# Small TensorE work at fixed steps, key products on GpSimd, and the last value pages outside TensorE, in a hybrid decoder step

## The chip, the cores and the metric

The kernel runs on one core of a Trainium2 chip. The metric is the device time of one execution, in microseconds. The time before the change is the median of three runs, 1570.15 us (1565.2 to 1571.04). PE is TensorE, DVE is VectorE, ACT is ScalarE, Pool (POOL in the rows, G in the code) is GpSimd, and SP is the queue that issues all transfers.

## What is computed

One layer of a decoder step over two inputs at once: a prompt of 512 tokens and eight sample sequences of one new token each. All data is 32-bit.

```
z = rmsnorm(x) @ w_in                      # 2048 -> 7168: q, k, v, gate_a, conv halves, gate_c
o = (softmax(q1 k1) - lam * softmax(q2 k2)) @ v      # 8 heads, two maps of 64 each
o_att  = rmsnorm(o) * silu(gate_a)
o_conv = (silu(layernorm(depthwise_conv31(glu))) @ w_pw) * silu(gate_c)
h = x + concat(o_att, o_conv) @ w_out
h = h + sigmoid(rmsnorm(h) @ w_pg) * (p @ w_ple)
y = rmsnorm(h)
```

For the prompt the keys and values are its own. For each of the eight samples they are 4096 cached positions, found through a page table as 32 pages of 128 positions, with 8 heads of 128 columns: a key page and a value page of 512 KB each. That makes 256 key pages and 256 value pages, some 268 MB of the 424 MB that the kernel moves.

## The kernel before

The program is straight-line code, and its order is worked out while it is built. A `Planner` keeps a predicted clock for each engine (`clk["PE"]`, `"V"` for DVE, `"A"` for ACT, `"G"` for Pool, `"Q"` for SP) and a predicted ready time of each tile. Every instruction goes through `Engine`, which records it at line 209 (so every row of the profile says L209; the tiles tell the rows apart).

The spine is a loop over slots (`run_slot`). A slot holds two 128-row blocks of a weight matrix, 512 columns wide, in one `raw` tile of 512 KB. ACT rounds each block to `hi`, Pool subtracts to get `lo = raw - hi`, and PE multiplies activations (split alike into `aht` and `alt`) with both: three matmuls for each of four token tiles, for each of the two blocks. This is the dense work, into the tiles `acc`. Three `hi`/`lo` pairs exist (`HIB`). After each three dense matmuls the loop calls `hook(n)`, with n from 0 to 7 within a slot. The hook issues loads (`wpump` for the slots' weights; `kring.pump`, `vring.pump` for pages), advances the queued generators in `tasks` (attention of the prompt, convolution, norms, softmax, sample work) as far as the planned clocks allow, and ends with `decode_tick(n)`. A generator that is about to use PE yields `on("PE", tiles)`, which holds it until the tiles are ready 500 ns before PE's planned clock.

`decode_tick` handles the pages. For a key page, DVE multiplies it in place with the query row `qb`, spread over 128 partitions, and the products are summed over 64 columns, either by one DVE reduce or, where DVE is planned more than 400 ns late, by sixteen ACT instructions with an accumulator (`k_act`). After 32 pages comes `softmax(s)`, which gives the weights `aw`. The keys of sequence s wait for the softmax of s - 2, and that softmax for the values of s - 4. For a value page, `v_pages` issues eight PE instructions (four column groups of 32 partitions) that add `aw x page` to the persistent PSUM tile `pers`; it takes them when two pages are there, or one at n = 7. `v_end(s)` gathers the result into `oS`.

Two rings hold pages: `kring` with five tiles (`kt`), `vring` with two (`vt`). The key ring takes keys as long as any are left, then values; the value ring takes values from the start. Both then take the `tail` pages: the weights of `w_out` and `w_pg` that the eight samples need after all their values are done (`sample_tail`, `tail_pass`). The slots' weights serve the samples too (`samp`, at n = 7 of every second slot, into `pers`). The last slots of `w_pg` wait until the samples have passed `w_out` (`us2_done`).

In the planner, Pool holds the SBUF port that it shares with DVE for each of its instructions, and so does a DVE instruction with two SBUF inputs. An instruction of one of them that meets one of the other is planned behind it.

Of the kernel before, what the change touches and what calls it, by code (L numbers as in the profile page):

```python
# [16 lines left out]
NSEQ = 8  # L17
# [43 lines left out]
class Planner:  # L61
# [4 lines left out]
    NEAR = dict(PE=0, V=125, A=125, G=60, Q=0)  # L66

    def __init__(self):
        self.t = dict(PE=0.0, V=0.0, A=0.0, G=0.0, Q=0.0, D=0.0)
        self.hist = {}  # L70
        self.late = dict(V=[], G=[])

# [88 lines left out]
    def put(self, eng, fn, args, kw, cost=None):  # L161
# [53 lines left out]
def hymba_step(ctx, tc, x_prompt, x_sample, p_prompt, p_sample, cache_k, cache_v, state_conv, page_table,  # L215
# [122 lines left out]

    def hook(n=7):
        wpump()  # L340
# [161 lines left out]
    def v_end(s):  # L502
# [7 lines left out]
        if vper[0] == s:  # L510
# [18 lines left out]
            yield from gather(ps)  # L529
        ended[0] += 1  # L530
# [6 lines left out]
    K_LATE = 400  # L537
# [8 lines left out]
    def decode_tick(at):  # L546
        if not dec["on"]:
            return
        now = clk["PE"]
        while True:  # L550
            more = k_next()
            pend = dec["pend"]
            if pend and (len(pend) > 1 or not more):
                s, pg, kt = pend[0]
                if k_act_live[0] < 1 and clk["A"] <= now + 300 and clk["V"] > now + K_LATE and plan.ready(kt) <= now + 800:
                    pend.pop(0)
                    k_act_live[0] += 1
                    spawn(k_act(s, pg, kt), rank=2)
                elif clk["V"] <= now + 400:
                    pend.pop(0)  # L560
                    V.tensor_reduce(out=dec["sc"][s][:, pg, :], in_=kt.rearrange("p (x d) -> p x d", d=64), axis=AX.X, op=ADD)
                    k_did(s, kt)
                else:
                    break
            elif more and clk["V"] <= now + 400:
                s, pg = divmod(dec["ik"], NPAGE)
                if pg == 0:
                    dec["sc"][s] = scp.tile([128, NPAGE, 16], F32, tag="sc", name="sc")
                kt, _ = kring.get()
                V.tensor_tensor(out=kt, in0=kt, in1=qbt[s], op=MUL)  # L570
                pend.append((s, pg, kt))
                dec["ik"] += 1
                if pg == NPAGE - 1 and s + 1 < NSEQ:
                    spawn(prep_qb(s + 1), rank=0)
            else:
                break
        v_pages(at == 7)
# [12 lines left out]

    def v_pages(tiled):

        n = v_here()
        if n < (1 if tiled else 2):
            return
# [11 lines left out]
        if vdone[s] == NPAGE:  # L607
            spawn(v_end(s), rank=0)
# [1114 lines left out]
```

## Time and profile before

| | |
|---|---|
| median of 3 runs | 1570.15 us (1565.2 to 1571.04) |
| the profiled execution, its own time | 1576.48 us |
| its span, first to last instruction | 1574.6 us |
| mean granted clock of TensorE | 0.978 |
| PE busy | 1482.9 us, 94% |
| DVE busy | 1100.8 us, 70% |
| ACT busy | 811.7 us, 52% |
| Pool busy | 622.9 us, 40% |
| moved | 424.40 MB, mean 270 GB/s |

Busy shares of the whole span hide the stages, so the rows below cut it where the work changes: the keys run until 1335 us, the last values until 1487 us, and behind that comes the samples' tail. The matmuls of PE overlap in the records: back-to-back dense matmuls start 0.234 us apart while each lasts 0.4 us. PE's work is therefore read from starts, not from durations.

### The profile page before, as it was taken

What the parts mean: (1) busy time and instruction counts of PE and PEld (TensorE: products, weight loads), DVE (VectorE), ACT (ScalarE), POOL (GpSimd) and SP (SyncE); (2) the same over time, 40 slices, a digit from 0 to 9 for tenths busy, and PEclk for the clock granted to TensorE, in tenths of its full rate; (3) what the DMA queues carried; (4) which work ended last, traced back from release to release, by engine and by line L of the source; (5) the groups of instructions that cost most, each with busy time, mean ns of one, the idle gap of its engine ahead of it and who ended that gap; (6) DMA issues with size and microseconds to landing.
All of it is one profiled execution on the core that took longest, in us unless ns stands there. A gap on an engine that the chain in (4) does not pass through costs nothing.

```text
span 1574.6 us, 32145 instructions
## 1 busy us (share of the span) xinstructions
PE 1482.9 (94%) x10448; PEld 1039.5 (66%) x10448; DVE 1100.8 (70%) x1636; ACT 811.7 (52%) x3810; POOL 622.9 (40%) x471
## 2 busy tenths in 40 slices
PE   5899999999999999999999999999999999999786
PEld 4676767666667766677777667766767777665453
DVE  5168987788798978888888868878867888301201
ACT  4156666556655645562445567665655765414202
POOL 5144534323333433344443454434423365425312
PEclk8999999999999999999999999999999999999877
DMA  7648779767887876543358687599878799899997
GB/s 287 233 169 294 273 257 358 275 228 256 320 282 279 296 251 207 188 135 124 126 168 295 228 307 254 187 350 340 299 258 332 275 327 382 306 328 337 395 320 255
DMA packets 148921, 424.40 MB, mean 270 GB/s; under 512 B 14192, under 2 KB 16226, under 8 KB 148480
## 3 DMA queue, kind: packets, MB, share of 16 engines
q1 hardware_dynamic: 148752, 422.35, 75.7%
q8 instruction: 82, 1.34, 0.3%
q14 instruction: 87, 0.71, 0.1%
HBM read 413.62 MB, written 9.63 MB: 269 GB/s over the span
## 4 chain that ended last, share of the span: by engine, by line
PE 75%; DMA 11%; DVE 5%; POOL 3%; issue 3%; ACT 2%; SPq 1%; POOLq 0%; ACTq 0%; DVEq 0%
PE acc L209 57%; PE pers L209 11%; PE misc L209 7%; DMA raw<-in_w_in_dram 4%; POOL lo L209 2%; DVE kt L209 1%; DMA raw<-in_w_out_dram 1%; DMA kt<-in_w_out_dram 1%; DMA raw<-in_w_pg_dram 1%; DVE bt L209 1%; DMA vt<-in_cache_v_dram 1%; DVE sc L209 1%; DMA kt<-in_w_pg_dram 1%; DMA kt<-in_cache_v_dram 0%; ACT hi L209 0%
## 5 line engine op out<-in xcount | busy, mean ns | idle before, releaser
L209 POOL TENSOR_TENSOR lo<-raw,hi 128x512 fp32r<-128x512 f32 x392 | 557.7, 1435 | 829.7 <-ACT hi L209 775.1
L209 ACT CAST hi<-raw 128x512 fp32r<-128x512 f32 x392 | 236.6, 618 | 437.1 <-PE acc L209 218.1
L209 DVE TENSOR_TENSOR kt<-kt,qb 128x1024 f32<-128x1024 f32 x256 | 363.9, 1436 | 41.1 <-DMA kt<-in_cache_k_dram 36.7
L209 PE MATMUL acc<-hi,aht 128*128 128x512 f32 x896 | 377.8, 422 | 7.8 <-ACT hi L209 7.5
L209 PE MATMUL acc<-lo,aht 128*128 128x512 f32 x896 | 360.9, 403 | 17.5 <-POOL lo L209 17.5
L209 PE MATMUL acc<-hi,alt 128*128 128x512 f32 x896 | 357.9, 399 | 0.2 <-DVE alt L209 0.2
L209 ACT ACTIVATE kt<-kt 128x64 f32<-128x64 f32 x1392 | 336.1, 244 | 25.2 <-DVE kt L209 25.2
L209 ACT ACTIVATION_READ_ACCUMULATOR kt<-kt 128x1 f32 x1392 | 262.2, 188 | 0.0
L209 PE MATMUL acc<-aht,hi 128*128 128x512 f32 x576 | 245.6, 426 | 3.9 <-DVE bt L209 3.4
L209 PE MATMUL acc<-aht,lo 128*128 128x512 f32 x576 | 228.8, 397 | 4.5 <-POOL lo L209 4.4
L209 PEld LDWEIGHTS acc<-hi,aht 128*128 128x128 f32 x896 | 170.2, 190 | 92.8 <-issue 32.4
L209 PE MATMUL acc<-alt,hi 128*128 128x512 f32 x576 | 227.5, 395 | 0.0
L209 PEld LDWEIGHTS acc<-lo,aht 128*128 128x128 f32 x896 | 170.7, 190 | 68.4 <-POOL lo L209 28.3
L209 DVE TENSOR_REDUCE sc<-kt 128x16 f32<-128x1024 f32 x169 | 203.4, 1210 | 1.3
L209 PEld LDWEIGHTS acc<-hi,alt 128*128 128x128 f32 x896 | 171.2, 191 | 33.3 <-DVE alt L209 0.7
L209 DVE SCALAR_TENSOR_TENSOR misc<-ft,wdwT,misc 128x512 f32<-128x512 f32 x240 | 180.3, 751 | 6.2
L209 PEld LDWEIGHTS acc<-aht,hi 128*128 128x128 f32 x576 | 108.5, 188 | 65.0 <-issue 34.3
L209 PEld LDWEIGHTS acc<-aht,lo 128*128 128x128 f32 x576 | 108.2, 188 | 34.8 <-POOL lo L209 9.2
L209 PEld LDWEIGHTS acc<-alt,hi 128*128 128x128 f32 x576 | 108.6, 189 | 18.0 <-issue 0.2
L209 PE MATMUL pers<-vt,aw 128*8 128x256 f32 x1624 | 113.4, 380 | 6.3 <-DVE pers L209 5.0
L209 DVE SCALAR_TENSOR_TENSOR acc<-acc,ct 128x512 f32<-128x512 f32 x16 | 11.2, 699 | 128.9 <-ACT acc L209 128.9
L209 PEld LDWEIGHTS pers<-vt,aw 128*8 128x8 f32 x1624 | 31.8, 88 | 62.9 <-issue 32.5
(259 smaller groups left out, 1283.2 us busy)
## 6 DMA issues: line engine op xcount, KB each, us to landing
kt<-in_cache_k_dram SPq DMA_DIRECT2D x256, 512.0 KB
vt<-in_cache_v_dram SPq DMA_DIRECT2D x203, 512.0 KB
raw<-in_w_in_dram SPq DMA_DIRECT2D x112, 512.0 KB
kt<-in_cache_v_dram SPq DMA_DIRECT2D x53, 512.0 KB
raw<-in_w_pg_dram SPq DMA_DIRECT2D x40, 512.0 KB
raw<-in_w_out_dram SPq DMA_DIRECT2D x32, 512.0 KB
kt<-in_w_in_dram SPq DMA_DIRECT2D x12, 512.0 KB
kt<-in_w_out_dram SPq DMA_DIRECT2D x12, 512.0 KB
```

The lines of the kernel that those rows point to most:

```text
L209: real(*args, **kw)
```

## The change

Three things are changed, and the planner's prices with them.

1. A PE step of a generator (`on("PE", ...)`) and `v_pages` go ahead only if `turn()` holds: at n = 3 and n = 7 of a slot, instead of at any n. In a `settle` (the loop waits for something) n counts as 7. The planner adds 92 ns whenever PE goes from dense to other work or back, and prices a group of four column-group matmuls at 226 ns instead of 284 ns, a value page at 431 ns instead of 430 to 580 ns.
2. `decode_tick` may give a key page's product to Pool: if DVE is planned more than 700 ns behind PE's clock, Pool's planned clock is at least 100 ns in the past, and fewer than three multiplied pages wait for their sums. Of the waiting pages it takes the first whose product is due within 700 ns, instead of the oldest.
3. When the last key page of the last sequence has been multiplied, the tile `qb` becomes an accumulator `vacc` for one sequence at a time. `v_aside` then takes arrived value pages: Pool multiplies one with its weights by one instruction with a broadcast operand, or ACT by eight (`v_act`), and DVE adds it to `vacc`. While this is possible, `v_pages` uses PE only if four pages are there. `v_end` sums `vacc` over partitions with sixteen more PE instructions.

The core of the diff:

```diff
+    TURN = 92
...
+            if eng == "PE":
+                dense = outs[0].name.startswith("acc")
+                c += self.TURN if dense != self.dense else 0
+                self.dense = dense
...
-        return lambda: (eng == "PE" or clk[eng] <= clk["PE"] + back) and all(plan.ready(x) <= clk["PE"] + back for x in aps)
+        return lambda: (eng != "PE" or turn()) and (eng == "PE" or clk[eng] <= clk["PE"] + back) and all(plan.ready(x) <= clk["PE"] + back for x in aps)
...
+    def turn():
+        return not main_on[0] or step[0] % TURNS == TURNS - 1
+    TURNS = 4
     def hook(n=7):
+        step[0] = n
...
+        if s in vacc:
+            ps = yield from take("misc")
+            V.memset(ps[:, 0:256], 0.0)
+            yield on("PE", ps[:, 0:256], vacc[s])
+            for h in range(8):
+                a, g = h // 4, h % 4
+                mm(ps[32 * g:32 * g + 8, a * 128:(a + 1) * 128], cst[:, C_ROW + 7 - s:C_ROW + 15 - s],
+                   vacc[s][:, h * 128:(h + 1) * 128], start=False, stop=True, cost=7 if g else 205)
+            va_free.append(plan.ready(vacc.pop(s), True))
+            yield from gather(ps)
...
-    K_LATE = 400
+    K_LATE, K_POOL = 400, -100
...
+            x = next((x for x in pend if plan.ready(x[2]) <= now + 700), None)
+            if x and (len(pend) > 1 or not more):
+                s, pg, kt = x
+                if k_act_live[0] < 1 and clk["A"] <= now + 300 and clk["V"] > now + K_LATE:
...
+            eng = V if clk["V"] <= now + 400 else G if clk["G"] <= now + K_POOL and clk["V"] > now + 700 and len(pend) < 3 else None
+            if eng is None:
+                break
...
-                V.tensor_tensor(out=kt, in0=kt, in1=qbt[s], op=MUL)
+            eng.tensor_tensor(out=kt, in0=kt, in1=qbt[s], op=MUL)
...
+            elif pg == NPAGE - 1:
+                va_free.append(plan.ready(qbt[s], True))
+        v_aside()
+        v_pages(at == 7)
...
+    def v_aside():
+        now = clk["PE"]
+        while v_pend and clk["V"] <= now + 500 and v_pend[0][0] in va_has and plan.ready(v_pend[0][1]) <= now + 600:
+            s, vt, ring = v_pend.pop(0)
+            V.tensor_tensor(out=vacc[s], in0=vacc[s], in1=vt, op=ADD)
+            ring.done(vt)
+            v_did(s)
+        while True:
+            ring = v_ring(600)
+            s, pg = divmod(dec["iv"], NPAGE)
+            if ring is None or not dec["soft"][s] or plan.ready(aw[s % 2]) > now + 500 or not (s in vacc or va_free) or len(v_pend) > 2:
+                return
+            eng = G if clk["G"] <= now + 200 else A if clk["A"] <= now + 300 and v_act_live[0] < 1 else None
+            if eng is None:
+                return
...
+            if eng is G:
+                a = aw[s % 2]
+                G.tensor_tensor(out=out.rearrange("p (h d) -> p h d", d=128), in0=vt.rearrange("p (h d) -> p h d", d=128),
+                                in1=a[:, pg, :].rearrange("p (h o) -> p h o", o=1).to_broadcast([128, 8, 128]), op=MUL, cost=1855)
+                v_made(s, vt, ring, first)
+            else:
+                v_act_live[0] += 1
+                spawn(v_act(s, pg, vt, ring, out, first), rank=2)
+    def v_act(s, pg, vt, ring, out, first):
+        for h in range(8):
+            c = slice(h * 128, (h + 1) * 128)
+            yield lambda: clk["A"] <= clk["PE"] + 400
+            A.activation(out=out[:, c], in_=vt[:, c], func=AF.Copy, scale=aw[s % 2][:, pg, h:h + 1])
...
+    V_MANY = 4
...
-        if n < (1 if tiled else 2):
+        if n < (V_MANY if s_aside() else 1 if tiled else 2) or not turn():
             return
...
-                   start=False, stop=True, cost=20 if cg else 370 + (0 if k or tiled else 150))
+                   start=False, stop=True, cost=7 if cg else 410)
```

## Rows read from the trace of the kernel before

**Rows 1.** The page, part 1: busy time, share of the span and instructions of an engine.

```profile
PE 1482.9 (94%) x10448; PEld 1039.5 (66%) x10448; DVE 1100.8 (70%) x1636; ACT 811.7 (52%) x3810; POOL 622.9 (40%) x471
```

**Rows 2.** The view by windows, cut by stage: the window, its length, busy us (instructions) of PE, PEld, DVE, ACT and POOL, the granted clock, the DMA share and GB/s.

```profile
82.00:560.00 478.00, 462.89 (x3089) 328.69 (x3088) 398.92 (x627) 280.00 (x1441) 186.26 (x137) 1.00 0.78 272
560.00:800.00 240.00, 233.20 (x1592) 166.86 (x1593) 199.24 (x384) 117.28 (x496) 92.48 (x77) 1.00 0.50 170
800.00:1000.00 200.00, 194.60 (x1271) 138.66 (x1269) 163.18 (x197) 117.59 (x565) 87.71 (x59) 1.00 0.71 245
1000.00:1335.00 335.00, 327.06 (x2067) 235.69 (x2066) 270.05 (x281) 207.99 (x1113) 144.50 (x98) 0.99 0.87 314
1335.00:1487.00 152.00, 144.04 (x1055) 87.54 (x1053) 27.32 (x54) 49.55 (x121) 66.84 (x54) 1.00 0.93 340
1487.00:1518.00 31.00, 19.59 (x298) 12.36 (x300) 5.80 (x19) 1.42 (x6) 1.35 (x2) 0.56 0.96 358
1518.00:1575.00 57.00, 40.95 (x570) 26.32 (x562) 8.22 (x18) 12.87 (x25) 14.40 (x13) 0.83 0.79 265
```

**Rows 3.** The view of waits for SP's queue, 82 to 1335 us: who waited for whom, us in total, times, longest us.

```profile
SPq L209 <- PE pers L209: 358.0, 117, 14.0
SPq L209 <- DVE sc L209: 73.2, 45, 12.4
```

**Rows 4.** The same view for PE, 82 to 1335 us.

```profile
PE acc L209 <- POOL lo L209: 12.3, 22, 1.4
```

**Rows 5.** Groups of instructions over the whole span, shapes kept apart: count, busy us, mean ns of one, then the idle time before them.

```profile
L209 POOL TENSOR_TENSOR lo<-raw,hi 128x512 fp32r<-128x512 f32 x392 | 557.7, 1435 | 829.7 <-ACT hi L209 775.1 <-PE acc L209 29.2 <-PE pers L209 20.9
L209 DVE TENSOR_TENSOR kt<-kt,qb 128x1024 f32<-128x1024 f32 x256 | 363.9, 1436 | 41.1 <-DMA kt<-in_cache_k_dram 36.7 <-ACT qb L209 3.5
L209 ACT ACTIVATE kt<-kt 128x64 f32<-128x64 f32 x1392 | 336.1, 244 | 25.2 <-DVE kt L209 25.2
L209 ACT ACTIVATION_READ_ACCUMULATOR kt<-kt 128x1 f32 x1392 | 262.2, 188 | 0.0
L209 DVE TENSOR_REDUCE sc<-kt 128x16 f32<-128x1024 f32 x169 | 203.4, 1210 | 1.3
L209 ACT ACTIVATE o<-misc,arz 128x128 f32<-128x128 f32 x32 | 11.8, 368 | 1.1
L209 POOL TENSOR_TENSOR ft<-ft,stat 128x512 f32<-128x512 f32 x6 | 6.3, 1066 | 0.0
```

**Rows 6.** The timeline of PE at three places: start us, us, instructions merged where equal.

```profile
701.86 0.27 PE L209 MATMUL misc<-cst,o 128*128 128x128 f32 x1
701.89 0.47 PE L209 MATMUL acc<-aht,hi 128*128 128x512 f32 x1
...
1340.50 0.40 PE L209 MATMUL acc<-hi,alt 128*128 128x512 f32 x1
1340.74 0.39 PE L209 MATMUL acc<-lo,aht 128*128 128x512 f32 x1
1341.06 1.05 PE L209 MATMUL pers<-vt,aw 128*8 128x256 f32 x16
1342.04 0.50 PE L209 MATMUL acc<-hi,aht 128*128 128x512 f32 x1
1342.38 0.40 PE L209 MATMUL acc<-hi,alt 128*128 128x512 f32 x1
...
1480.49 0.62 PE L209 MATMUL pers<-kt,aw 128*8 128x256 f32 x8
1480.92 0.61 PE L209 MATMUL pers<-vt,aw 128*8 128x256 f32 x8
```

**Rows 7.** The timeline of PE, 444 to 470 us: the first and the last of the five stretches of value pages in it.

```profile
446.71 1.07 PE L209 MATMUL pers<-vt,aw 128*8 128x256 f32 x16
...
467.95 1.05 PE L209 MATMUL pers<-vt,aw 128*8 128x256 f32 x16
```

**Rows 8.** The view by windows for the instructions that touch the softmax weights `aw` (on PE, eight for each value page): the window, its length, busy us (instructions) of PE, PEld and DVE, then granted clock, DMA share and GB/s of everything.

```profile
505.00:657.00 152.00, 17.35 (x256) 5.17 (x256) 0.43 (x1) 1.00 0.68 237
657.00:814.00 157.00, 0.00 (x0) 0.00 (x0) 0.41 (x1) 1.00 0.42 140
814.00:962.00 148.00, 17.54 (x256) 5.38 (x256) 0.00 (x0) 1.00 0.80 279
962.00:1017.00 55.00, 0.00 (x0) 0.00 (x0) 0.14 (x1) 1.00 0.49 161
...
1335.00:1487.00 152.00, 39.83 (x600) 12.37 (x600) 0.42 (x1) 1.00 0.93 340
```

**Rows 9.** The view by tile for `qb`, 1325 to 1340 us: instruction, count, ns min/median/max, first and last start us, shapes.

```profile
L209 DVE TENSOR_TENSOR kt<-kt,qb x5: 1216/1217/1373, 1325.4 to 1333.8; 128x1024 f32<-128x1024 f32 x5
```

**Rows 10.** The timeline of all engines near 990 us, where the slots of `w_pw` need the end of the layer norm.

```profile
990.06 0.50 PE L209 MATMUL acc<-aht,hi 128*128 128x512 f32 x1 [2.54 <-DVE bt L209]
...
991.59 1.38 POOL L209 TENSOR_TENSOR lo<-raw,hi 128x512 fp32r<-128x512 f32 x1 [3.33 <-ACT hi L209]
...
991.74 2.31 DVE L209 TENSOR_TENSOR kt<-kt,qb 128x1024 f32<-128x1024 f32 x1
```

**Rows 11.** The timeline of PE behind the last dense matmul before the samples' tail.

```profile
1485.12 0.62 PE L209 MATMUL pers<-kt,aw 128*8 128x256 f32 x8 [2.72 <-DMA kt<-in_cache_v_dram]
...
1505.26 1.04 PE L209 MATMUL misc<-kt,mST 128*8 128x128 f32 x16 [2.16 <-DMA kt<-in_w_out_dram]
```

More of the change, by code (lines that the diff above doesn't have):

```diff
@@ L549, in decode_tick @@
         now = clk["PE"]
+        pend = dec["pend"]
         while True:
             more = k_next()
[L552 to L556, printed above, removed]
+            x = next((x for x in pend if plan.ready(x[2]) <= now + 700), None)
+            if x and (len(pend) > 1 or not more):
+                s, pg, kt = x
+                if k_act_live[0] < 1 and clk["A"] <= now + 300 and clk["V"] > now + K_LATE:
+                    pend.remove(x)
@@ L557, in decode_tick @@
                     k_act_live[0] += 1
                     spawn(k_act(s, pg, kt), rank=2)
[L559 to L560 removed]
+                    continue
+                if clk["V"] <= now + 400:
+                    pend.remove(x)
                     V.tensor_reduce(out=dec["sc"][s][:, pg, :], in_=kt.rearrange("p (x d) -> p x d", d=64), axis=AX.X, op=ADD)
                     k_did(s, kt)
[L563 to L569, printed above, removed]
[L570 to L576 removed]
@@ L577, in decode_tick @@
-        v_pages(at == 7)
+                    continue
+            if not more:
+                break
+            eng = V if clk["V"] <= now + 400 else G if clk["G"] <= now + K_POOL and clk["V"] > now + 700 and len(pend) < 3 else None
+            if eng is None:
+                break
+            s, pg = divmod(dec["ik"], NPAGE)
+            if pg == 0:
+                dec["sc"][s] = scp.tile([128, NPAGE, 16], F32, tag="sc", name="sc")
+            kt, _ = kring.get()
+            eng.tensor_tensor(out=kt, in0=kt, in1=qbt[s], op=MUL)
@@ new lines, in decode_tick @@
+            pend.append((s, pg, kt))
+            dec["ik"] += 1
+            if pg == NPAGE - 1 and s + 1 < NSEQ:
+                spawn(prep_qb(s + 1), rank=0)
+            elif pg == NPAGE - 1:
+                va_free.append(plan.ready(qbt[s], True))
+        v_aside()
+        v_pages(at == 7)
+    va_free, vacc, va_has, v_act_live, v_pend = [], {}, set(), [0], []
+    def v_aside():
[13 more added lines that the diff above has]
+                return
+            first = s not in vacc
+            if first:
+                vacc[s] = plan.begin(qbp.tile([128, 1024], F32, tag="qb", name="qb"), va_free.pop(0))
+            vt, _ = ring.get()
+            dec["iv"] += 1
+            out = vacc[s] if first else vt
+            if eng is G:
[3 more added lines that the diff above has]
+                v_made(s, vt, ring, first)
+            else:
+                v_act_live[0] += 1
+                spawn(v_act(s, pg, vt, ring, out, first), rank=2)
@@ L579, in v_here, with v_did, v_ring @@
+    def v_did(s):
+        vdone[s] += 1
+        if vdone[s] == NPAGE:
+            spawn(v_end(s), rank=0)
+    def v_ring(ahead=0):
+        best = min((r for r in (kring, vring) if r.tiles and r.tiles[0][1] == VALS), key=lambda r: r.tiles[0][2], default=None)
+        return best if best and best.tiles[0][2] == dec["iv"] and plan.ready(best.tiles[0][0]) <= clk["PE"] + ahead else None
     def v_here():
@@ L598, in v_pages @@
         for k in range(n):
-            ring = kring if kring.here(VALS) and (not vring.here(VALS) or kring.tiles[0][2] < vring.tiles[0][2]) else vring
+            ring = v_ring()
+            if ring is None:
+                break
             vt, idx = ring.get()
```

23 lines of the change are left out of this document (17 added, 6 removed).

## The prediction, as it was put on record

> **What bounds the kernel now.** I read the busy shares first and then cut them by stage, because the totals mislead: PE is at 94%, DVE at 70%, Pool at 40% [rows 1], and this looks like a kernel bound by PE alone. The windows show three regimes [rows 2]. Until 1335 us, while there are keys, PE is busy 97 to 98% of each window (462.89 of 478, 327.06 of 335) and DVE 81 to 84%, while the transfers reach only 170 to 314 GB/s. From 1335 to 1518 us DVE is almost idle and the transfers run at 340 and 358 GB/s, a share of 0.93 to 0.96: here the bytes set the pace. After 1518 us comes the rest of the samples' weights and a short chain without transfers. The timeline confirms the middle part: PE, out of dense work, waits 2.72 us for a value page and 2.16 us for a `w_out` page [rows 11].
>
> So the end is set by bytes that come late, and they come late because pages are used up too slowly before. The waits of SP's queue name who holds the ring tiles: value pages that PE has not yet multiplied, 358 us in all, and key pages that DVE has not yet summed, 73.2 us [rows 3]. Value pages also stop altogether for 157 and 55 us [rows 8], when the softmax of the next sequence has to wait for its keys. DVE is thus the engine behind the late bytes. A key page costs it (363.9 + 203.4)/256 = 2.22 us on average, since ACT sums 1392/16 = 87 of the 256 pages [rows 5].
>
> **The gathered PE work.** A stretch of two value pages between dense matmuls costs 1342.38 - 1340.74 - 2 x 0.234 = 1.17 us, with 0.24 us between dense starts before it. Pages inside a stretch start 0.43 us apart, so a stretch costs 1.17 - 0.86 = 0.31 us beside its pages. A lone transpose costs nothing of the kind: the next dense matmul starts 0.03 us after it [rows 6]. So only stretches of column-group work are worth joining, and the planner's 92 ns for every other step has no counterpart. Five stretches lie between 446.71 and 467.95 us, mostly of two pages [rows 7]. From 216 to 1335 us PE takes 256 - 75 = 181 pages (75 from 600/8 [rows 8]), some 100 stretches. Now they may begin only at two of eight steps, and every fourth of these has the samples' weight work of every second slot. If a third joins, 33 x 0.31 = 10 us of PE; ends are 0 and 31 us. The cost of the wait for a turn: a step of a chain starts up to 2.8 us later (twelve matmuls of 0.234 us), 1.4 us on average. What is queued behind it is the chain's own next step on DVE or ACT. Only one chain has no slack: the layer norm, for which PE already waits 2.54 us at 990 us [rows 10]. It has about six PE steps; I charge 5 us (0 to 9).
>
> **Key products on Pool.** The trace has no Pool instruction of 1024 columns. The nearest is the split of 512, 1.38 us where it runs freely and 1.435 on average [rows 5, 10]; a product of twice the size lies between that and twice 1.435, 2.87 us. I take 2.5, nearer to the double. Pool's idle time before 1000 us is 918 - (186 + 92 + 88) = 552 us, and 335 - 144.5 = 190 us to 1335 [rows 2]. The ends are no page and 552/2.5 = 220, more than there are keys by then. The conditions (Pool free, DVE 700 ns late, a page landed, fewer than three waiting for sums) must all hold at one of the steps, and DVE is 81 to 84% busy, so they hold often but not mostly. I take a quarter: 55 pages before 1000 us, 20 after.
>
> Each relieves DVE of a multiplication of 1.436 us on average, 1.217 where nothing is in its way [rows 5, 9]. Against it stands the port: the multiplication at 991.74 us took 2.31 us, behind a Pool split that began 0.15 us earlier [rows 10]. The mean excess today is 1.436 - 1.217 = 0.22 us per multiplication; for Pool instructions twice as long I charge 0.6 us of DVE per page. Net 55 x (1.436 - 0.6) = 46 us, which at 2.22 us is 20 more key pages by 1000 us, or 10.5 MB (0.524 each). Sequences' keys then end earlier by about an eighth, which shortens the 212 us without value pages [rows 8]; at 32 pages in 152 us some 80 us would be 17 pages, but a pair of value pages now waits for its turn, so I count half, 4 MB. Against 14 MB I count 13. The split may be late behind a product; PE waits for `lo` only 12.3 us in 22 waits [rows 4], and three pairs hold 8.4 us of dense work, so I charge nothing here and keep it as a rival.
>
> **The last value pages outside PE.** From 1335 to 1487 us PE spends 39.83 us on 75 pages, 0.53 us each [rows 8]. If 40 go aside, 21 us less, minus sixteen instructions more per sequence, about 1 us each. It lies beside a stage bound by bytes, so I cost it at nothing on the path; the cover are transfers at 340 GB/s [rows 2]. If those were not in the way it would be worth up to 20 us. The new work has room: Pool with a broadcast operand took 1.066 us for 512 columns, so about 2.1 for a page; ACT with eight pieces at 0.244 to 0.368, 2.0 to 2.9 [rows 5]; DVE adds 1.2; DVE is 18% busy there, ACT 33%, Pool 44% [rows 2]. A ring tile is held some 3 us longer, and the last page is later by about that; I charge 2 us.
>
> **The sum.** Bytes after 1000 us: 335 x 0.314 + 152 x 0.340 + 31 x 0.358 + 57 x 0.265 = 183 MB [rows 2]. The last window has 57 - 15.1/0.358 = 15 us without transfers. With keys no longer holding them back, the transfers should run from 1000 us as they do at 1335 to 1518; 0.358 is the best window, 0.325 the mean from 1335 to the end, and I take 0.335. In MB per us, 1000 + (183 - 13)/0.335 + 15 + 5 + 2 = 1529 us, against a span of 1574.6: 45 us less. The profiled run took 1576.48, 6.3 above the median of 1570.15; I subtract from the median and predict 1525 us. PE does not stand in the way: its dense work ends near 1482 now and would end 30 us earlier by the terms above.
>
> **Rivals.**
> 1. *Pool gets next to no keys*, because its planned clock is rarely 100 ns in the past when DVE is late. For it: three splits often stand in a row. Against it: 742 us of idle Pool before 1335. Then the last key stays near 1335 us with 78 MB behind it [rows 2], and of the gathered 10 us only what brings the slots' weights forward counts, about half: 1565 us, no change.
> 2. *Slower: the port.* Each Pool product blocks a DVE multiplication. Its place is the key stage, the price the part of 2.5 us for which DVE stands still; it decides from 1.436 us on, where the move costs DVE more than it saves. At 2.0 us, 75 pages cost 75 x 0.56 = 42 us of DVE, which at 82% busy puts the last key 51 us later. Meanwhile transfers go on at the slowest window's 0.170 MB per us, 8.7 MB, and these are missing behind it: 8.7/0.325 = 27 us. So 51 - 27 + 5 + 2 = 31 us more, about 1601 us. For it: the 2.31 us. Against it: 169 sums of 1.210 us [rows 5], with one SBUF input each, give DVE other work meanwhile. The Trainium skill, "SBUF — State Buffer", on the sides of SBUF, says the pair of ports is an exclusive lock held for a whole instruction and that the loser fully blocks. The row at 991.74 us agrees (2.31 against 1.217). By that rule alone, with every product meeting one of DVE's, this rival would hold, and at the full 2.5 us the sum would be higher still.
> 3. *Late splits.* Pool's product stands before a split that PE needs. At 0.5 us for each of 75, 37 us of waits; half of it is covered by the stage bound by bytes: about 1546 us, still faster.
>
> **How the numbers follow.** My forecast (1492 to 1545) 0.6, rival 3 (1545 to 1560) 0.14, rival 1 0.13, rival 2 0.1, better than 1492 0.03. The low end has 18 MB moved ahead and 0.345 MB per us: 1000 + 165/0.345 + 22 = 1500 us of span, 1496 in the metric, and 4 us for PE work that is not covered. The high end, 1580, takes in rivals 1 and 3 and leaves out rival 2. A difference of 0.5%, 8 us, is about what a measurement can tell here. Faster 0.76, same 0.13, slower 0.11.
>
> **What would show it.** Right: 50 to 100 key products on POOL, the last key before 1290 us, fewer stretches of `pers` on PE, GB/s over 330 from 1000 us on, and value pages on Pool and ACT after the keys. Wrong: DVE products of 2.5 to 3.7 us in number (rival 2), PE waits for `lo` of over 30 us (rival 3), or the last key at 1335 still (rival 1). The largest uncertainty is the number of pages that Pool takes; next is whether values keep up when they may be multiplied at two steps of eight only.

## The result and the profile after

The changed kernel is slower: a median of 1579.13 us (1573.23 to 1591.54, twelve runs) against 1566.85 us (1561.43 to 1571.94, twelve runs) of the kernel before, a ratio of 1.0085 with a 95% interval of 1.0066 to 1.0103. The time lies just inside the range, at its upper end, and on the side to which the prediction gave 0.11. The profiled execution of after has a span of 1581.6 us, with a mean granted clock of 0.973. That execution is 4 us above the median of its kernel, and the one of before, 1576.48 us, is 10 us above its median, so differences of a few us between the two profiles are not to be leaned on.

The page of after, part 1, then its windows, with the columns of [rows 2] (the last ends 7 us later):

```profile
PE 1457.9 (92%) x10088; PEld 1047.8 (66%) x10088; DVE 1136.0 (72%) x1544; ACT 919.5 (58%) x4370; POOL 1004.7 (64%) x628
```

```profile
82.00:560.00 478.00, 445.65 (x2902) 325.01 (x2903) 398.29 (x571) 297.53 (x1634) 301.73 (x187) 0.97 0.75 267
560.00:800.00 240.00, 226.16 (x1620) 156.15 (x1622) 206.46 (x380) 150.06 (x786) 164.41 (x104) 0.99 0.73 249
800.00:1000.00 200.00, 192.63 (x1384) 133.79 (x1384) 168.04 (x194) 125.03 (x691) 141.04 (x81) 1.00 0.82 287
1000.00:1335.00 335.00, 316.39 (x1993) 234.53 (x1993) 255.38 (x239) 209.07 (x945) 234.60 (x129) 0.97 0.83 297
1335.00:1487.00 152.00, 144.44 (x1099) 105.42 (x1098) 63.58 (x72) 79.05 (x205) 88.11 (x59) 0.99 0.78 269
1487.00:1518.00 31.00, 30.09 (x316) 19.37 (x315) 0.17 (x1) 9.72 (x17) 15.86 (x14) 1.00 0.91 302
1518.00:1582.00 64.00, 41.16 (x253) 29.30 (x252) 13.27 (x29) 22.39 (x43) 26.59 (x24) 0.81 0.39 130
```

Two things stand here together. The bytes did move ahead, and by more than predicted: before 1000 us the first three windows move 127.6 + 59.8 + 57.4 = 245 MB, against 130.0 + 40.8 + 49.0 = 220 MB in [rows 2]. The last key page is done at 1204 us instead of 1335. The transfers are no longer what the end waits for: 269 GB/s from 1335 us and 130 GB/s, at a share of 0.39, in the last window. And yet PE finishes later: from 1480 us on it still has some 220 dense matmuls to do, where before had some 70, and its last one ends at 1566 us instead of 1560.

A ledger of PE says where the time is. A span is PE's busy time plus PE's idle time. Busy fell by 1482.9 - 1457.9 = 25.0 us [rows 1]; idle rose from 91.7 to 123.7 us, by 32.0. The difference is the 7.0 us by which the span grew. Nearly all of the added idle time lies in the key stage: from 82 to 1335 us PE is idle for 1253 - 1217.8 = 35 us before [rows 2] and 1253 - 1180.8 = 72 us after. Behind 1335 us it is idle for 35 us before and 31 us after. So the question is who made PE wait in the key stage, and why the earlier bytes bought nothing.

Groups of after, with the columns of [rows 5]:

```profile
L216 POOL TENSOR_TENSOR kt<-kt,qb 128x1024 f32<-128x1024 f32 x136 | 337.3, 2486 | 61.5 <-DMA kt<-in_cache_k_dram 45.0 <-ACT qb L216 14.7 <-PE pers L216 1.1
L216 DVE TENSOR_TENSOR kt<-kt,qb 128x1024 f32<-128x1024 f32 x120 | 186.7, 1568 | 42.2 <-DMA kt<-in_cache_k_dram 36.7 <-ACT qb L216 5.2
L216 DVE TENSOR_TENSOR qb<-qb,kt 128x1024 f32<-128x1024 f32 x35 | 69.6, 1989 | 13.3 <-ACT kt L216 5.8 <-DMA vt<-in_cache_v_dram 2.1 <-issue 2.0
L216 DVE TENSOR_SCALAR o<-o,oq 128x128 f32<-128x128 f32 x32 | 37.6, 1178 | 13.1 <-POOL oq L216 12.8 <-issue 0.3
L216 DVE TENSOR_TENSOR rt<-tmp,cst 128x128 f32<-128x128 f32 x32 | 20.4, 676 | 1.0 <-ACT tmp L216 1.0
```

Pool takes 136 key pages at 2.486 us (75 at 2.5 were predicted). What the prediction did not look at are small DVE steps of the prompt: `o<-o,oq` belongs to its attention, `rt<-tmp,cst` to the rotation of its queries and keys ahead of that. The same two groups in the kernel before:

```profile
L209 DVE TENSOR_SCALAR o<-o,oq 128x128 f32<-128x128 f32 x32 | 14.0, 441 | 8.1 <-POOL oq L209 8.0
L209 DVE TENSOR_TENSOR rt<-tmp,cst 128x128 f32<-128x128 f32 x32 | 12.4, 429 | 6.4 <-ACT tmp L209 6.2
```

They grow from 441 and 429 ns to 1178 and 676 ns.

The waits of PE and of SP's queue in after, 82 to 1335 us, with the columns of [rows 3]:

```profile
PE pers L216 <- DMA vt<-in_cache_v_dram: 20.1, 11, 7.3
PE misc L216 <- DVE tmp L216: 9.7, 4, 4.6
PE acc L216 <- POOL lo L216: 8.5, 13, 1.3
PE pers L216 <- DVE pers L216: 7.3, 7, 3.5
PE misc L216 <- DVE ppS L216: 6.1, 1, 6.1
```

```profile
SPq L216 <- PE pers L216: 261.8, 91, 13.0
SPq L216 <- DVE sc L216: 138.1, 57, 15.4
```

The wait for the splits, rival 3's place, fell from 12.3 to 8.5 us [rows 4]. The new waits are for value pages (20.1 us; 1.4 before) and for DVE's results: all rows of PE that name DVE come to 31.8 us, 11.8 before. SP's queue waits less for value pages to be multiplied, but 138.1 us instead of 73.2 for key tiles that DVE has not yet summed [rows 3].

The timeline of after shows how such a wait comes about, in some instructions of DVE, Pool and SP's queue from 499 to 518 us (start, us, merged count):

```profile
499.39 0.49 DVE L216 TENSOR_TENSOR rt<-tmp,cst 128x128 f32<-128x128 f32 x2
499.92 0.36 DVE L216 TENSOR_TENSOR tmp<-rt 128x64 f32<-128x64 f32 x2
...
503.55 2.40 POOL L216 TENSOR_TENSOR kt<-kt,qb 128x1024 f32<-128x1024 f32 x1
504.54 2.86 DVE L216 TENSOR_TENSOR rt<-tmp,cst 128x128 f32<-128x128 f32 x2
505.90 1.35 POOL L216 TENSOR_TENSOR lo<-raw,hi 128x512 fp32r<-128x512 f32 x1
507.21 2.44 POOL L216 TENSOR_TENSOR kt<-kt,qb 128x1024 f32<-128x1024 f32 x1
507.43 2.44 DVE L216 TENSOR_TENSOR tmp<-rt 128x64 f32<-128x64 f32 x2
509.79 4.70 DVE L216 SCALAR_TENSOR_TENSOR misc<-ft,wdwT,misc 128x512 f32<-128x512 f32 x6
...
514.40 2.34 DVE L216 TENSOR_REDUCE sc<-kt 128x16 f32<-128x1024 f32 x2
515.64 0.34 SPq L216 DMA_DIRECT2D kt<-in_cache_k_dram  x1
516.81 1.50 SPq L216 DMA_DIRECT2D vt<-in_cache_v_dram  x2
```

The same two pairs of DVE steps are seen twice. At 499 us they take 0.49 and 0.36 us; at 504 us each begins behind the start of a Pool product, ends after it, and takes 2.86 and 2.44 us. The Trainium skill, "SBUF — State Buffer", on its two sides, says that whoever loses the pair of ports stands until the other's instruction is over, and these rows agree: the first pair, begun at 504.54, is over only after Pool has ended its product at 505.95 and a split, a kind of step that the kernel before has too, at 507.25. Together the four steps take 4.5 us more of DVE than at 499 us. Behind them in DVE's order stand six steps of the convolution and then the sums of two key pages; the first sum, over at about 515.6 us, frees the key tile for which SP's queue has stood 15.4 us (the longest wait of the row above); only then does SP issue the next key page and, behind it, two value pages. Meanwhile the transfers are down to 2 GB/s (505 to 514.4 us). One of the two value pages is what PE waits for. So as these rows read, the port accounts for at most 4.5 of the 15.4 us, and the order in which DVE and SP take their work for the rest. The timeline of PE in after behind this place, and its windows (columns of [rows 2]):

```profile
521.77 1.04 PE L216 MATMUL pers<-vt,aw 128*8 128x256 f32 x8 [7.34 <-DMA vt<-in_cache_v_dram]
524.62 0.63 PE L216 MATMUL acc<-hi,alt 128*128 128x512 f32 x1
525.05 0.63 PE L216 MATMUL acc<-lo,aht 128*128 128x512 f32 x1
...
527.40 0.39 PE L216 MATMUL acc<-lo,aht 128*128 128x512 f32 x1
527.63 0.40 PE L216 MATMUL acc<-hi,aht 128*128 128x512 f32 x1
```

```profile
520.00:524.00 4.00, 1.98 (x16) 0.24 (x16) 1.22 (x1) 0.00 (x0) 1.58 (x1) 0.50 0.88 306
524.00:527.20 3.20, 3.20 (x12) 2.51 (x9) 0.00 (x0) 0.62 (x1) 1.28 (x1) 0.51 1.05 421
527.20:532.00 4.80, 4.80 (x22) 3.88 (x21) 4.66 (x6) 3.64 (x23) 1.40 (x2) 1.00 1.02 409
```

A wait is paid twice. The granted clock is 1.00, the 2.4 GHz level, while PE works on from 510 to 514.4 us; then PE stands for 7.34 us, and from 520 to 527.2 us the clock is 0.50 to 0.51, the 1.2 GHz level, and dense matmuls start 0.43 us apart; then it is 1.00 again, and they start 0.23 us apart.

### The profile page after: what moved, and what is told of

Same layout as the page of the kernel before. It is cut to its first block, busy times and chain, and to the rows that moved or that the text cites. A ratio compares the mean times of both kernels' runs of the same rounds, so it can differ in the third digit from the quotient of the medians.

```text
span 1581.6 us, 32181 instructions
## 1 busy us (share of the span) xinstructions
PE 1457.9 (92%) x10088; PEld 1047.8 (66%) x10088; DVE 1136.0 (72%) x1544; ACT 919.5 (58%) x4370; POOL 1004.7 (64%) x628
## 5 line engine op out<-in xcount | busy, mean ns | idle before, releaser
L216 ACT ACTIVATE kt<-kt 128x64 f32<-128x64 f32 x1552 | 374.6, 245 | 26.0 <-DVE kt L216 18.7
L216 POOL TENSOR_TENSOR kt<-kt,qb 128x1024 f32<-128x1024 f32 x136 | 337.3, 2486 | 61.5 <-DMA kt<-in_cache_k_dram 45.0
L216 ACT ACTIVATION_READ_ACCUMULATOR kt<-kt 128x1 f32 x1552 | 293.6, 189 | 0.0
L216 DVE TENSOR_TENSOR kt<-kt,qb 128x1024 f32<-128x1024 f32 x120 | 186.7, 1568 | 42.2 <-DMA kt<-in_cache_k_dram 36.7
L216 DVE TENSOR_REDUCE sc<-kt 128x16 f32<-128x1024 f32 x159 | 189.7, 1210 | 19.2 <-POOL kt L216 18.2
L216 PE MATMUL pers<-vt,aw 128*8 128x256 f32 x1488 | 103.5, 384 | 27.5 <-DMA vt<-in_cache_v_dram 20.1
```

The costliest lines, as they stand in the source:

```text
L216: real(*args, **kw)
```

## The experiments

All ratios are to the kernel before, run beside each kernel on the same chip; the brackets are 95% intervals. "Idle" is PE's idle time from 82 to 1335 us in the profiled execution, length less busy time by the windows (35 before, 72 after). Expectations that speak of PE's waits as 42 us for the kernel before and 73 us with the Pool products alone counted them in another way; by the windows these are 35 and 61 us.

**The change with one part left out.** Without the Pool products:

```diff
-    K_LATE, K_POOL = 400, -100
+    K_LATE, K_POOL = 400, -1e9
```

> The changed kernel with one constant altered, so that no key product goes to Pool; gathered PE work and the value pages outside TensorE stay. Theory A (the Pool products hold the port that DVE shares, DVE's steps come late against the plan, and with them ring tiles, loads and PE): PE's waits fall from some 106 us back to about 80, the keys end near 1330 us again, and the end is bound by late bytes: ratio to the kernel before 0.990 to 1.002. Theory B (the gathered steps and their new prices cost the time): the ratio stays at 1.005 or above. Theory C (PE is now the bound to the end and the three parts only move work about): 1.000 to 1.008, with PE waits of 90 us or more.

Measured: 1.0096 [1.0064, 1.0129], 1579.67 us; no product on Pool, last key 1290 us, idle 30 us. The key stage's idle time is that of before again, so it belongs to the Pool products. The time doesn't fall with it: a new wait of 41.8 us stands behind 1335 us (e9 below). So the ratio above 1.005, which theory B asked for, does not speak for theory B; e5 and e6 decide on that.

Without the gathered steps and their prices:

```diff
-    TURN = 92
+    TURN = 0
...
-    TURNS = 4
+    TURNS = 1
...
-                       cost=7 if g else 205)
+                       cost=20 if g else 214 + 10)
...
-                   start=False, stop=True, cost=7 if cg else 410)
+                   start=False, stop=True, cost=20 if cg else 370 + (0 if k or tiled else 150))
```

> The changed kernel with PE steps allowed at all eight steps of a slot and with the planner's old prices; Pool products and value pages outside TensorE stay. Theory A: the waits stay, some 190 to 230 stretches of column-group work return at 0.31 us: ratio 1.008 to 1.015. Theory B: the waits of PE for value pages and for DVE's results vanish, ratio 0.970 to 0.995.

Measured: 1.0019 [0.9999, 1.0039], 1567.07 us; idle 55 us. Gathering with its prices, in company of the Pool products, makes the kernel slower by 0.7%; e4 and e18 show that the prices do it.

Without the pages aside:

```diff
-            elif pg == NPAGE - 1:
-                va_free.append(plan.ready(qbt[s], True))
```

> The changed kernel without the value pages outside TensorE (the accumulator is never given out); gathered work and Pool products stay. If PE is the bound to the end, as the short tail of the changed kernel suggests, the 51 pages come back to PE at 0.43 to 0.53 us, 22 to 27 us, less about 6 us of instructions that sum the accumulators: ratio 1.018 to 1.024. If the pages aside do not matter, 1.006 to 1.011. Theories A and B do not differ here.

Measured: 1.0246 [1.0204, 1.0288], 1604.05 us; idle 71 us. So the pages aside gain 1.6% within the change. Without them PE's busy time is 1482.2 us, with them 1457.9: the 24 us are those of the 51 pages (21 on Pool, 30 on ACT) that leave PE, less the 48 instructions that sum the accumulators.

The turns kept and the planner's prices put back (first e4, all prices; then e18, the 92 ns alone):

```diff
-    TURN = 92
+    TURN = 0
...
-                       cost=7 if g else 205)
+                       cost=20 if g else 214 + 10)
...
-                   start=False, stop=True, cost=7 if cg else 410)
+                   start=False, stop=True, cost=20 if cg else 370 + (0 if k or tiled else 150))
```

> The changed kernel with the planner's old prices for PE work (no 92 ns at a change of kind, 284 ns a group, 430 to 580 ns a value page); the steps are still gathered. Theory A: no effect beyond chance, 1.005 to 1.012. Theory B in the form that the new prices take away a cushion (the old plan had PE faster than it is, so everything else was early): PE's waits for value pages fall from 20 us to under 5 and the ratio to 0.990 to 1.000.

Measured: 1.0008 [0.9985, 1.0031], 1566.53 us; idle 58 us.

```diff
-    TURN = 92
+    TURN = 0
```

> The changed kernel with the 92 ns taken out and the cheaper prices of groups and pages kept. If the 92 ns, which no row supports for lone transposes, is what makes the plan of PE slower than PE and so lets pages be late: ratio back to 0.998 to 1.004, PE's waits for value pages from 20 us to 12 or less. If the cheaper groups are the cause: 1.006 to 1.014. If the 0.8% is only another order of the same work, anything between 0.995 and 1.015 with waits that do not follow either price.

Measured: 1.0003 [0.9978, 1.0027], 1567.17 us; idle 65.5 us. By these intervals the 92 ns are the whole 0.8% that the prices cost in this company, and the other prices do nothing; in the kernel before they cost nothing (e5 against e6). The waits of PE in e18 (82 to 1335 us) show the value pages on time more often, 10.3 instead of 20.1 us, while other rows grow (the profiled execution of e18, 1577.67 us, is the longest of its twelve):

```profile
PE pers L216 <- DVE pers L216: 18.7, 10, 6.9
PE pers L216 <- DMA vt<-in_cache_v_dram: 10.3, 7, 3.2
```

**One part alone.** The gathered steps with their prices, in the kernel before, and then the turns without the prices:

```diff
-        return lambda: (eng == "PE" or clk[eng] <= clk["PE"] + back) and all(plan.ready(x) <= clk["PE"] + back for x in aps)
+        return lambda: (eng != "PE" or turn()) and (eng == "PE" or clk[eng] <= clk["PE"] + back) and all(plan.ready(x) <= clk["PE"] + back for x in aps)
...
-        if n < (1 if tiled else 2):
+        if n < (1 if tiled else 2) or not turn():
```

> The kernel before with the first part alone: PE steps and value pages at two of eight steps, and the new prices. Theory B now reads: the new prices make the planned PE slower at each change of kind, so pages and results are due later in the plan than they are wanted, and PE waits for them. It expects PE waits in 82 to 1335 us above the 42 us of before (50 to 75) and 1.003 to 1.010. Theory D (the prices only hurt together with Pool's products, which make DVE late): waits of 42 to 48 us, some 30 stretches fewer, 0.993 to 1.001.

> The kernel before with the gathered steps alone and the old prices. Both theories expect no new waits; 20 to 40 stretches fewer are 6 to 12 us of PE, of which the end, bound by bytes, hides most: 0.994 to 1.001. If gathering itself made chains late, PE waits in 82 to 1335 us would rise by 10 us or more and the ratio be above 1.003.

Measured: e5 0.9875 [0.9844, 0.9905], 1546.88 us; e6 0.9885 [0.9857, 0.9913], 1549.71 us. The windows of e5:

```profile
82.00:1335.00 1253.00, 1224.32 (x8227) 878.63 (x8227) 1026.87 (x1490) 765.21 (x3993) 509.69 (x369) 0.99 0.77 272
1335.00:1620.00 285.00, 183.45 (x1690) 119.16 (x1688) 35.68 (x70) 60.26 (x119) 83.53 (x70) 0.96 0.62 217
```

Its span is 1542.6 us, 32 shorter: 12.5 us of PE's busy time and 19.5 of its idle time. This is the fastest kernel here that computes everything, faster than both that were given. The last key is done at 1293 us; ACT sums 98 pages instead of 87. The stretches of column-group work fall only from some 226 to some 220 (207 in e6), separate small stretches of any kind from 389 to 323 (301 in e6).

The Pool products alone, in a kernel without turns, new prices and pages aside (the edits of e2 and e3 on the changed kernel):

> The changed kernel with Pool's key products alone: no gathered steps, old prices, no value pages outside TensorE. Theory A' (the port: Pool's products of 2.4 us hold up small DVE steps whose results PE wants): PE waits in 82 to 1335 us rise from 42 to 60 to 70 us, the end gives some 15 to 25 us back: 0.998 to 1.012. By the sum of the prediction, with 130 products instead of 75, it would be 0.95 to 0.97.

Measured: 1.0159 [1.0132, 1.0185], 1592.73 us; 125 products; last key 1236 us. Groups and window of e7:

```profile
L216 POOL TENSOR_TENSOR kt<-kt,qb 128x1024 f32<-128x1024 f32 x125 | 319.2, 2562 | 43.5 <-DMA kt<-in_cache_k_dram 28.2 <-ACT qb L216 12.7 <-DVE sc L216 2.3
L216 DVE TENSOR_TENSOR kt<-kt,qb 128x1024 f32<-128x1024 f32 x131 | 209.6, 1611 | 55.7 <-DMA kt<-in_cache_k_dram 47.8 <-ACT qb L216 4.4 <-ACT hi L216 3.0
L216 DVE TENSOR_SCALAR o<-o,oq 128x128 f32<-128x128 f32 x32 | 27.1, 848 | 13.2 <-POOL oq L216 11.3 <-ACT hi L216 1.9
```

```profile
82.00:1335.00 1253.00, 1192.05 (x8203) 833.33 (x8202) 966.52 (x1371) 724.01 (x3761) 764.41 (x465) 0.98 0.80 280
```

The keys end 99 us earlier and the kernel is 25 us slower. Idle is 61 us. DVE's busy time over the span is 1032.3 us against 1100.8 [rows 1]: 68.5 us less, of which ACT's five more sums are 6. So 125 products bring DVE some 62 us, 0.50 each, where 1.436 less 0.6 was counted. And here it is plain what PE waits for: the rows that name DVE come to 37.6 us (11.8 before), those for value pages to 6.0 us (1.4 before), those for splits to 8.0 us (12.3 before). So the 26 us that are added are, on balance, waits for DVE's results.

The pages aside alone (the edits of e1 and e2 on the changed kernel):

> The changed kernel with the value pages outside TensorE alone: no gathered steps, old prices, no key product on Pool. The keys end near 1335 us again and the end is bound by bytes: by the prediction PE's 20 to 25 us are worth nothing there, 0.997 to 1.003. If holding the pages for Pool, ACT and the sums on DVE slows the ring, as in the run without Pool, where PE waited 42 us for the last sums, 1.003 to 1.015.

Measured: 1.0319 [1.0287, 1.0352], 1617.59 us. Window, one row of PE's waits behind 1335 us, and the timeline of Pool and DVE in e8:

```profile
1487.00:1530.00 43.00, 0.00 (x0) 0.00 (x0) 41.55 (x19) 0.00 (x0) 37.71 (x14) 0.50 0.63 193
```

```profile
PE misc L216 <- DVE tmp L216: 68.6, 1, 68.6
```

```profile
1487.81 5.71 POOL L216 TENSOR_TENSOR vt<-vt,aw 128x1024 f32<-128x1024 f32 x2
1489.02 8.41 DVE L216 TENSOR_TENSOR qb<-qb,kt 128x1024 f32<-128x1024 f32 x3
1493.48 11.38 POOL L216 TENSOR_TENSOR kt<-kt,aw 128x1024 f32<-128x1024 f32 x4
```

PE does nothing for 43 us on end while Pool and DVE handle page after page at about 2.8 us each on either engine. As long as the accumulator is in use, `v_pages` takes PE only for four pages at once, and with PE out of dense work nothing else would use them.

**Was the end bound by bytes?** The kernel before with a quarter of each value page loaded:

```diff
-                    SP.dma_start(out=t, in_=(ck if kind == KEYS else cv)[bass.ds(pg, 1)].rearrange("o p d -> (o p) d"))
+                    c = 1024 if kind == KEYS else 256
+                    SP.dma_start(out=t[:, 0:c], in_=(ck if kind == KEYS else cv)[bass.ds(pg, 1)].rearrange("o p d -> (o p) d")[:, 0:c])
-                mm(pers[32 * cg:32 * cg + 8, 0:256], aw[s % 2][:, idx % NPAGE, :], vt[:, cg * 256:(cg + 1) * 256],
+                mm(pers[32 * cg:32 * cg + 8, 0:256], aw[s % 2][:, idx % NPAGE, :], vt[:, 0:256],
```

> The kernel before, but each value page is loaded with 256 of its 1024 columns, and the four column groups on PE all read these; PE's work is the same, some 100 MB are not moved, and the sample attention is computed from a part of the values. The prediction took the end to be set by late bytes: then some 100 MB less, at 0.335 MB per us, should take off far more than 45 us, 0.93 to 0.97. Theory P (PE's own work of some 1484 us and its waits elsewhere set the time, and earlier bytes can save only the waits of the last 240 us, 35 us less some 18 that remain): 0.983 to 0.997.

Measured: 0.9831 [0.9807, 0.9855], 1540.29 us, with some 256 x 0.393 = 101 MB less to move. Windows of e12:

```profile
82.00:1335.00 1253.00, 1227.15 (x8331) 870.26 (x8330) 1031.50 (x1502) 726.39 (x3642) 524.79 (x367) 1.00 0.62 207
1335.00:1620.00 285.00, 179.46 (x1593) 120.32 (x1593) 33.81 (x75) 61.71 (x121) 85.48 (x72) 0.96 0.44 152
```

In the prediction's sum the 75 late pages alone are 29.5 MB, at 0.335 MB per us 88 us. The kernel gains 25. Its ratio lies outside the 0.93 to 0.97 of an end set by bytes and at the lower edge of theory P's range. Its PE is busy for 1468.6 us and idle for 72: with the transfers at 152 GB/s behind 1335 us, PE's own work still fills the span.

**What in the Pool products costs, and can it be avoided?** Each product as two instructions of 512 columns, on e7:

```diff
-            eng.tensor_tensor(out=kt, in0=kt, in1=qbt[s], op=MUL)
+            for c in ((slice(0, 512), slice(512, 1024)) if eng is G else (slice(0, 1024),)):
+                eng.tensor_tensor(out=kt[:, c], in0=kt[:, c], in1=qbt[s][:, c], op=MUL)
```

> Pool's key products alone, as before in the run of that part, but each product issued as two instructions of 512 columns, so that Pool holds the port for 1.3 us at a time and not for 2.4. Theory A' (small DVE steps wait behind the whole Pool instruction): DVE's blocked time outside the key products falls from 136 us towards 90, PE's waits in 82 to 1335 us from 73 to 50 to 62 us, ratio from 1.016 to 1.003 to 1.010. If the products cost by the order of loads or by the plan, no change: 1.013 to 1.020.

Measured: 1.015 [1.0117, 1.0183], 1589.28 us, 112 pages, 1.462 us for a half; idle 54 us. A shorter hold changes nothing that can be told from e7. All the products together take Pool as long as in e7 (322.2 against 319.2 us).

No product on Pool while an attention unit of the prompt is under way, in the changed kernel (e11) and in e7 (e17):

```diff
-            eng = V if clk["V"] <= now + 400 else G if clk["G"] <= now + K_POOL and clk["V"] > now + 700 and len(pend) < 3 else None
+            eng = V if clk["V"] <= now + 400 else G if all(att_next[p] == 16 - att_left[p] for p in (0, 1)) and clk["G"] <= now + K_POOL and clk["V"] > now + 700 and len(pend) < 3 else None
```

> The changed kernel, but no key product goes to Pool while a unit of the prompt's attention is under way. Theory A': PE's waits for DVE's and ACT's results of that attention (tmp, o: some 25 us) go, keys end some 40 us later than in the changed kernel, ratio from 1.0085 to 0.992 to 1.003. If the products cost the same wherever they stand, the ratio falls only in proportion to their number: 1.004 to 1.010.

> Pool's key products alone (old prices, no gathered steps, no pages aside), but none while a unit of the attention is under way. With all of them the ratio was 1.016 and PE waited 73 us in 82 to 1335 us (before: 42). If they cost by what DVE does beside them: fewer products, some 75 of 125, PE's waits 42 to 55 us, ratio 0.998 to 1.006. If they cost by number: 75/125 of 1.6%, 1.008 to 1.012, waits 58 to 66 us.

Measured: e11 1.0022 [1.0000, 1.0044], 81 products, idle 57 us; e17 1.0132 [1.0098, 1.0165], 87 products, idle 54.5 us. By number alone e17 would cost 87/125 x 1.59 = 1.1%, which its interval holds. It holds the whole 1.6% of e7 too, so a cost by number fits but is not proven. What e17 does exclude is its first theory, 0.998 to 1.006, and with it the steps of the attention as the main cause: `o<-o,oq` is back at 281 ns in e17 (848 in e7), `rt<-tmp,cst` stays at 696 ns, PE's waits for DVE's results stay at 26.2 us, and the kernel stays slow.

The planner made to let a PE step wait until its inputs are 2 us old, in e7 (e13), in the changed kernel (e14) and in e5 (e15):

```diff
-        back = -500.0 if eng == "PE" else 500.0
+        back = -2000.0 if eng == "PE" else 500.0
```

> Pool's key products alone, with the margin before a PE step 2000 ns instead of 500 ns (a step goes ahead only when its input is planned ready 2 us before). If the waits come from results later than planned by up to one Pool instruction: PE's waits in 82 to 1335 us fall from 73 to 45 to 58 us, DVE's share of them most, and the ratio from 1.016 to 1.000 to 1.009. If they come from ring tiles and loads: 1.013 to 1.020, waits 68 us or more.

> The changed kernel with the margin of 2000 ns. By the first cause PE's waits for DVE's and ACT's results (some 35 of 82 us in 82 to 1335 us) halve, those for value pages (23 us) stay: ratio from 1.0085 to 0.995 to 1.003. By the second 1.005 to 1.012.

> The gathered steps and new prices alone (0.9875) with the margin of 2000 ns: a control. Without Pool's products the waits for DVE are small (35 us in all in 82 to 1335 us, half of them for splits), so a wider margin should give nothing: 0.983 to 0.992. If it slows the chains, above 0.992.

Measured: e13 1.0174 [1.0142, 1.0207], e14 1.0165 [1.0132, 1.0199], e15 0.9954 [0.9937, 0.9972]. In e13 PE's waits for DVE fall from 37.5 to 23 us, but those for splits, ACT and transfers rise; idle is 57 instead of 61 us. The margin slows e14 and e15 and leaves e13 where e7 was. That a chain which is kept waiting brings a lateness of its own would explain it, but is not shown.

PE allowed to take value pages again when the loop has nothing else, and none started aside meanwhile, on e1 (e9), and the same together with the edits of e11 and e14 on the changed kernel (e16):

```diff
-            if ring is None or not dec["soft"][s]
...
+            if waiting[0] or ring is None or not dec["soft"][s]
...
-        if n < (V_MANY if s_aside() else 1 if tiled else 2) or not turn():
+        if n < (V_MANY if s_aside() and not waiting[0] else 1 if tiled else 2) or not turn():
```

> As the run without Pool's key products (gathered steps, new prices, value pages outside TensorE), but while the loop waits, pages go to PE again, one at a time, and none aside. In that run PE waited 41.8 us at one place for the last sums of DVE while pages went through Pool and DVE one by one. If the rule that PE takes pages only by four, kept up while PE has nothing else, was the cost: the wait falls below 12 us and the ratio from 1.0096 to 0.980 to 0.992. If the pages aside cost by holding ring tiles, so that loads come late, 1.000 to 1.010.

> The changed kernel with what helped: the margin of 2000 ns, no key product on Pool while the attention is under way, and value pages on PE while the loop waits. If the parts' effects add up, 1.0085 less 0.6% (attention), less some 0.8% (margin), less a little for the idle PE: 0.985 to 0.997, still not better than the gathered steps alone at 0.9875.

Measured: e9 0.9968 [0.9945, 0.9992], 1558.88 us: the wait of 41.8 us is gone and the idle time behind 1335 us falls from 77 to 46 us, against 24 in e5. The 1.3% that this edit brings are the price of keeping pages from PE while PE has nothing else; what is left is still 0.9% slower than e5, which leaves the pages to PE. e16 measured 1.0118 [1.0082, 1.0153]: with the margin in it (e14, 1.0165), the other two edits bring back about half a per cent and the kernel stays slower than before.

## Why the prediction was wrong

**The step that failed** is the sum: "with keys no longer holding them back, the transfers should run from 1000 us as they do at 1335 to 1518", and with it "PE does not stand in the way". The end was taken as set by late bytes. 25 MB went ahead, twice the 13 predicted, and the last key came at 1204 us where "before 1290" was asked for; the end did not follow. From 1000 us on the transfers reach 297, 269 and 302 GB/s, not the 335 of the sum: from 1000 to 1487 us SP's queue stands 107 us for tiles that PE has to free (68.7 for `pers`, 38.2 for `misc`) and 83 us for tiles that DVE has to (55.3 for the sums of the pages aside, 28.0 for key sums). e12 tests the bytes: 101 MB less are worth 25 us. So it is PE that sets most of the time of the kernel before, at 94% busy [rows 1], and in the stage from 1335 us, with its 340 GB/s, PE was busy 144 of 152 us as well [rows 2]. Of the 35 us of PE's idle time behind 1335 us, 24 to 26 remain in e5, e7 and e12, so of idle time about 10 us were there to be won by earlier bytes; the profiled span of e12 is 34 us shorter, and the rest of that are 9 us of idle time in the key stage and 14 us of PE's busy time, at a mean granted clock of 0.989 instead of 0.978.

A ledger of PE would have tested the sum beforehand. By the prediction's own terms, with the sums of three sequences, PE is busy for 1482.9 - 10 - 21 + 3 = 1455 us, and 1457.9 were measured. A span of 1529 us therefore left 74 us for all of PE's idle time, where before had 91.7 and after has 123.7. The total of the busy part came true, in part by luck (without the pages aside, in e3, it is 1482.2 us, so the 10 us of the gathered steps are not in it); it is the idle time that decides.

**The price of a Pool product on PE was missing.** Its duration was right (2.486 against 2.5 us), its number too low (136 against 75), its charge on DVE too small (0.94 us by e7 against 0.6). Rival 2 named the port, but its place was the key stage's length, and the keys became faster, not slower. Rival 3 named PE waits, but for the splits, and these fell (its own sum, 1525 plus half of 37, gives 1543.5 us and not 1546). What happened lies between: with the products on Pool, DVE's results for other chains come late, late key tiles hold SP's queue and with it value pages, and PE stands, 37 us more in after (20 for DVE's results, 19 for value pages, less elsewhere) and 26 in e7, there nearly all for DVE's results; the granted clock of the windows falls with it, from 1.00 to 0.97 in the first of them. Alone the products cost 1.6%. The runs fit a cost that goes with the number of products (e7, e17) but do not prove it. A product of two halves keeps the cost (e10), so the length of one hold is not the point. Why DVE's results come late, whether by the port itself or by the order of DVE's work that late key tiles bring about, is not shown: no run occupies Pool without a key tile changing hands.

**The pages outside PE were costed at nothing on the path but 2 us, and that was wrong both ways.** With Pool products the keys end early, PE is behind, and they gain 1.6% (e3): the "up to 20 us" that the prediction kept for the case of no cover. Without them the keys end late, PE is idle while pages go through Pool and DVE one by one, and they cost 3.2% (e8) or, on top of the gathered steps, 2.2% (e1 against e5). The prediction's "The new work has room" compared busy shares; the rows show Pool and DVE taking turns, 2.8 us a page on each.

**The gathered steps were under-sized.** 10 us were counted on PE, but the sum has none of them, only the 5 us charged for the layer norm; e5 gains 20 us (1.25%), e6 18. The mechanism was only partly the predicted one: the joins of column-group stretches, which were to be a third of a hundred, are some 7 to 19 of 226. Of the 32 us in e5's span 12.5 are PE's busy time, the rest idle time before and behind 1335 us. Why the keys end 42 us earlier with it (eleven more sums on ACT) stays open. In company of the Pool products the turns gain nothing (e4 against e2), and the 92 ns cost 0.8% (e18).

**The parts don't add.** The three alone are -1.25, +1.6 and +3.2%, together +0.85%. In pairs they are +2.46 (e3, first and second), +0.96 (e1, first and third) and +0.19% (e2, second and third). The second moves the keys out of the third's way, and together these two cost next to nothing; the second takes the first's gain, and with the 92 ns in the plan more than that.

## What to carry to other kernels

Before a sum is built on late bytes, ask what PE does at the same time: where it is 94% busy, take bytes away in one run and see whether the end moves. Work given to an idle engine is not free when results that the busiest engine waits for come later through it; the price then appears as idle time of the busiest engine, far from the work that was moved. Changes that shift the same wait are to be run alone and in pairs before they are kept together: here only one of three gains anything alone.

## What the runs showed of the hardware that was not expected

A DVE step of 128 columns that takes 0.44 us in the kernel before takes 1.18 us on average in after, with 136 Pool products of 2.49 us, and 0.85 us in e7, with 125; in e17, whose 87 products keep away from the attention, it takes 0.28 us. Over e7, a Pool product that spares DVE 1.436 us leaves it only 0.50 us better off. A PE wait of 7.34 us was followed by 3 us at half the clock, in which dense matmuls started 0.43 instead of 0.235 us apart. Transfers reach more than the 358 GB/s of the best stage of before: by part 2 of its page, a slice of 39 us near 1476 us has 395 GB/s. (The 409 and 421 GB/s of the windows of 3 to 5 us above stand at shares over 1.0, so these windows are too short to be read as rates.)
